# Five-slice feed-forward products: a named place for every weight and split buffer, and a low part ordered behind the first sum

## The chip, the cores and the metric

One Trainium2 chip, one of its cores. The metric is the device time of one execution in microseconds (us). The kernel before takes 1798.35 us, the median of three runs (1797.55 to 1800.99).

## The reference

A decoder block on x (256 tokens, width 2048, float32): a SwiGLU feed-forward of width 5632 added at half weight, a mixer, a second feed-forward, a final norm. The change is about the feed-forwards:

```
def swiglu_ffn(x, w_gate, w_up, w_down):
    return (jax.nn.silu(x @ w_gate) * (x @ w_up)) @ w_down

x = x + 0.5 * swiglu_ffn(rms_norm(x, ffn1_norm), ffn1_w_gate, ffn1_w_up, ffn1_w_down)
z = rms_norm(x, mix_norm) @ w_in            # mixer: two head groups read z
x = x + y @ w_out                           # y: the two normalised groups
x = x + 0.5 * swiglu_ffn(rms_norm(x, ffn2_norm), ffn2_w_gate, ffn2_w_up, ffn2_w_down)
return rms_norm(x, final_norm)
```

## The kernel before

**How a weight is multiplied.** TensorE takes float32 as fp32r, so every weight tile is split in two: `parts_of` (L242) lets ScalarE cast it to fp32r in two pieces (the high part, `hi`), and VectorE subtract (the low part, `lo`). A product of a tile needs two passes with `hi` and one with `lo` for each slice of 128 rows. The weights come from HBM by DMAs issued on SP's queue. All instructions that go through the wrapper of an engine carry line 43 in the profile, so they are told apart by their tiles.

**A product of seven.** `seven` (L454) multiplies a quadrant block of weights w11, w12, w21, w22 (each some slices of 128 rows by 512 columns) with seven products in place of eight, p0 to p6, in the manner of Strassen and Winograd. Beside them stand plain products of further rows, x01, x11, x00, x10, with the weights b2, b3, a2, a3. Sums of weights are formed in place: VectorE adds w12 to w11 (the first sum, L499), then w22 (L524), then w21. GpSimd issues accumulating DMAs, w12 += w22 (L502), in two pieces where there are more than four slices. Only p6 reads that sum. There are four banks of sums, a, c, e, d. The order on TensorE is p0 into a, p4 into c, x01, p5 into a, x11, p6 into a, p2 into c, x00, p3 into a, x10, p1 into d. ScalarE takes snapshots of the banks between products: s1 and u2, u3 of a, and s5 of c, which must be taken before x01 and x11 add into c.

**Stages.** Each feed-forward runs through s = 0 to 4. In stage 0 a gate and an up product run over tall quadrants of four slices (three split pairs). In stages 1 and 2, and again 3 and 4, the quadrants are five slices tall and the plain products three (the "fine" stages, `tall` and `short`, two split pairs). After stages 0, 2 and 4 a down stage uses what was made. So there are 16 five-slice products: in each feed-forward the gate and up products of stages 1 and 2 (a block), a down stage, those of stages 3 and 4 (a second block), and a down stage. The names in the trace are `g`, `u` and `d` with the suffix `_p` for the seven and `_x` for the plain ones.

**Places.** The code asks for buffers from pools of the tile framework. `open_stage` (L184) opens one pool on each side of the on-chip memory; `raw_tile` (L195) takes a weight's place under a tag with two or three buffers ("kept" for w11 and w12, "raw", or "tall" and "short" in the fine stages), and `split_tiles` (L223) takes a pair of hi and lo. Within a tag, the buffer that comes free first is given out; the load into it waits for its last readers. Instructions of an engine are put into an order by the framework's scheduler, except where the kernel asks for program order (`held`, `pinned`).

```
        product_of(0, w11, a, True)
        dve.tensor_tensor(w11, w12, w11, op=ALU.add)
        for h in (slice(0, UK), slice(UK, w12.shape[1])):
            if h.start < h.stop:
                nc.gpsimd.dma_start(w12[:, h, :], w22[:, h, :], accum_op=ALU.add)
        ...
        product_of(4, w11, c, True)
        ...
        s5 = snap(c, "s5")
        ...
        usual(0, b2, 1, (e, 1, True, not two), (c, 0, False, False), first=blk)
```

Of the kernel before, what the change touches and what calls it, by code (L numbers as in the profile page):

```python
# [23 lines left out]
CW = 512  # L24
NC_D = D // CW
UK = 4
NH = 8
# [22 lines left out]
def hybrid_block(ctx: ExitStack, tc: tile.TileContext, a: dict, out: bass.AP):  # L50
    nc = tc.nc
    Engine.pinned = False
    dve, act, pe, sp = (Engine(tc, e) for e in (nc.vector, nc.scalar, nc.tensor, nc.sync))
# [24 lines left out]
    bigs = ctx.enter_context(tc.tile_pool(name="bigs", bufs=10, side="left"))  # L78
# [7 lines left out]
    def f32(ap):  # L86
        return ap.bitcast(F32)
# [82 lines left out]
    def big(name):  # L170

        return bigs.tile([P, UK, 2 * S], F32R, tag="big", name=name)
# [2 lines left out]

    extra = []
    turn_of = {"split": 0}
    stage = {"count": 0}

    def more_from(pool):  # L180
        extra.append(pool)
        turn_of["split"] = 0

    def open_stage(pairs, fine=False):  # L184

        n = stage["count"] = stage["count"] + 1
        for side in ("left", "right"):
            stage[side] = tc.alloc_tile_pool(name=f"stage{n}_{side}", bufs=1, side=side, reuse_waits="tile")
        stage.update(pairs=pairs, fine=fine)

    def close_stage():
        for side in ("left", "right"):
            stage[side].release()

    def raw_tile(name, rows, kept):  # L195
        if kept and extra:
            pool, tag, bufs = (bigs, "big", 10) if extra[0] is bigs else (extra[0], "kept", 2)
        elif kept:
            pool, tag, bufs = stage["right"], "kept", 2
        elif not stage["fine"]:  # L200
            pool, tag, bufs = stage["right"], "raw", 3
        else:
            pool, tag, bufs = stage["right"], "tall" if rows > UK else "short", 2
        return pool.tile([P, rows, CW], F32, tag=tag, name=f"raw_{name}", bufs=bufs)

    def load(src, name, pieces=((0, UK),), loaded=None):
        raw = raw_tile(name, UK, False)
# [6 lines left out]
    def gather(w, cs, runs, name, kept=False):  # L214

        raw = raw_tile(name, sum(n for _, n in runs), kept)
        at = 0
        for k, n in runs:
            sp.dma_start(raw[:, at : at + n, :], w[k * P : (k + n) * P, cs].rearrange("(j p) c -> p j c", p=P))
            at += n  # L220
        return raw

    def split_tiles(name, rows=UK):  # L223
        both = ("hi", "lo")
        if stage["fine"] and rows < UK:
            return [big(f"{part}_{name}")[:, :rows, :] for part in both]
        pool, bufs = stage["left"], stage["pairs"]
        if extra:
            turn_of["split"] += 1
            if turn_of["split"] % 3 == 0:  # L230
                if extra[0] is bigs:
                    return [big(f"{part}_{name}") for part in both]
                pool, bufs = extra[0], 1
        return [pool.tile([P, rows, CW], F32R, tag=part, name=f"{part}_{name}", bufs=bufs) for part in both]

    def low_part(raw, hi, lo):
        dve.tensor_tensor(lo, raw, f32(hi), op=ALU.subtract)

    def blocks(hi, lo):
        return [(hi[:, j, :], lo[:, j, :]) for j in range(hi.shape[1])]  # L240

    def parts_of(raw, name):  # L242
# [211 lines left out]
    def seven(w, rows, cols, sf, xs, name, keep, done, between=None, early=False, own=None, factor=None):  # L454
# [14 lines left out]
        def get(runs, n, kept=False):  # L469
            return gather(w, slice(cols[n], cols[n] + CW), runs, f"{name}_{runs[0][0]}{n}", kept)  # L470
# [16 lines left out]
        def usual(i, raw, n, *targets, first=None):  # L487

            blk = first or parts_of(raw, f"{name}_x{i}{n}")
            if own:  # L490
                last = i == len(xs) - 1
                targets = [(apart[t, n], t, i == 0, last) for t in range(NT)]
            multiply([(ps, xs[i][1](t), b, z) for ps, t, b, z in targets], blk, True)
            if own and last:
                for t in range(NT):
                    own(t, n, apart[t, n])

        product_of(0, w11, a, True)
        dve.tensor_tensor(w11, w12, w11, op=ALU.add)  # L499
        for h in (slice(0, UK), slice(UK, w12.shape[1])):  # L500
            if h.start < h.stop:
                nc.gpsimd.dma_start(w12[:, h, :], w22[:, h, :], accum_op=ALU.add)  # L502
# [3 lines left out]
        blk = None  # L506
        if early:
            between("second product")
            hi, lo = split_tiles(f"{name}_x01")
# [4 lines left out]
            blk = blocks(hi, lo)  # L514
# [13 lines left out]
        blk = blk2 = None  # L528
        if early:
            blk = parts_of(b3, f"{name}_x11")  # L530
# [29 lines left out]
        done(0, 0, d, [s1])  # L560

    def ffn(tag, norm, after, opening=False):
        with tc.tile_pool(name=f"ffn{tag}", bufs=1, side="left") as fp:
            wg, wu, wd = (a[f"ffn{tag}_w_{s}"][0] for s in ("gate", "up", "down"))

            def keep(name, dt=F32):
                return fp.tile([P, CW], dt, tag="keep", name=name, bufs=11)

            def spare_tile(name, dt=F32):
                return stage["right"].tile([P, CW], dt, tag="spare", name=name, bufs=2)  # L570

            open_stage(3)

            hidden = {}
            turned = {}
# [98 lines left out]
            left = []  # L674
# [265 lines left out]
            for s in range(5):  # L940
                cs = (CW + 2 * s * CW, 2 * CW + 2 * s * CW)
# [54 lines left out]
                if s == 0:  # L996
                    fifth()
                else:
                    if s % 2 == 0:
                        close_stage()  # L1000
                        open_stage(3)
                if s % 2 == 0:
                    down(s == 4)
            close_stage()
# [45 lines left out]

    acc = const.tile([P, 2, S], F32, name="acc")
    yT, yv = [], []
    open_stage(2)
    with tc.tile_pool(name="mixer", bufs=1, side="left") as mp, tc.tile_pool(name="mixw", bufs=2, side="left") as mw:
        wgate = {}

        def gate_weights(key, src):
            raw = stage["right"].tile([P, NH, P], F32, tag="raw", name=f"rawgate_{key}", bufs=3)
# [9 lines left out]
        zx, gv, hs, vs, ds, ts, cc, ys, yh, xcs = ({} for _ in range(10))  # L1068

        def tmp(tag, name, w=S, dt=F32, bufs=2):  # L1070
            return mw.tile([P, w], dt, tag=tag, name=f"{tag}_{name}", bufs=bufs)

        def halves(ps, name):

# [151 lines left out]
        def sc_c(between):  # L1226
# [35 lines left out]
                    turn(1)  # L1262

            c0 = 3 * (D // 2)
            more_from(bigs)
# [33 lines left out]
        behind = None  # L1299
        for i, (use, part, half) in enumerate(order):  # L1300
            ps = columns(w_in, part * (D // 2) + half * CW, nm.xT, f"in_{part}_{half}", behind)
            behind = None
            if i == 0:
# [5 lines left out]
                behind = sc_c(lambda: use(ps, half))  # L1309
# [28 lines left out]
        n2.later(0)  # L1338


    with tc.tile_pool(name="outs", bufs=1, side="left") as op:
        more_from(op)

        def snapshot(name):
            return op.tile([P, CW], F32, tag="snap", name=name, bufs=4)

        so = {}
        pair = [big(f"ys_{i}") for i in range(2)]
# [40 lines left out]
        extra.clear()  # L1389
    close_stage()  # L1390


    fss = const.tile([P, NT, NC_D], F32, name="fss")
# [96 lines left out]
```

## Time and profile before

| | |
|---|---|
| time, median of 3 | 1798.35 us |
| the profiled execution | 1795.43 us |
| its span | 1793.7 us |
| mean granted clock of TensorE | 0.988 |
| TensorE busy | 1734.6 us, 97% |
| VectorE busy | 1500.4 us, 84% |
| ScalarE busy | 1088.8 us, 61% |
| bytes moved by DMA | 376.81 MB, 210 GB/s |

A row of a timeline gives the start, the duration (of several instructions in a row, "x4", from the first start to the last end), the engine, the line, the operation, the tile written and the tiles read, the shape, and in brackets the idle time of the engine before it with what ended it. A row of the waits gives the total, the number and the longest. A row of the stretches gives the busy time of each engine in a stretch of the span, TensorE's granted clock, the DMA engines' share and GB/s. Matmuls are pipelined: a group's time runs past the start of the next one, so the pitch is read from start to start.

### The profile page before, as it was taken

What the parts mean: (1) busy time and instruction counts of PE and PEld (TensorE: products, weight loads), DVE (VectorE), ACT (ScalarE), POOL (GpSimd) and SP (SyncE); (2) the same over time, 40 slices, a digit from 0 to 9 for tenths busy, and PEclk for the clock granted to TensorE, in tenths of its full rate; (3) what the DMA queues carried; (4) which work ended last, traced back from release to release, by engine and by line L of the source; (5) the groups of instructions that cost most, each with busy time, mean ns of one, the idle gap of its engine ahead of it and who ended that gap; (6) DMA issues with size and microseconds to landing.
All of it is one profiled execution on the core that took longest, in us unless ns stands there. A gap on an engine that the chain in (4) does not pass through costs nothing.

```text
span 1793.7 us, 20426 instructions
## 1 busy us (share of the span) xinstructions
PE 1734.6 (97%) x7937; PEld 1428.7 (80%) x7937; DVE 1500.4 (84%) x1226; ACT 1088.8 (61%) x1408; POOL 47.7 (3%) x78
## 2 busy tenths in 40 slices
PE   9999799999999999999999989999899999999998
PEld 8888688788788788888888868887678788787776
DVE  7988689889589888787997878897889885998896
ACT  7665366556465656667866656654566563656564
POOL 0100000000000000000000000000000000000000
PEclk9999899999999999999999999999999999999999
DMA  8774586656677665565556555673877576877483
GB/s 305 244 241 150 179 279 200 217 202 202 221 226 228 205 223 176 211 189 191 184 189 223 179 187 186 217 252 127 273 236 220 154 236 211 268 222 235 125 274 118
DMA packets 181586, 376.81 MB, mean 210 GB/s; under 512 B 7412, under 2 KB 10352, under 8 KB 177776
## 3 DMA queue, kind: packets, MB, share of 16 engines
q1 hardware_dynamic: 174656, 340.81, 54.5%
q0 software_dynamic: 6656, 33.63, 10.0%
q8 instruction: 62, 1.02, 0.2%
q10 hardware_dynamic: 176, 1.06, 0.1%
q14 instruction: 36, 0.29, 0.0%
HBM read 339.82 MB, written 2.10 MB: 191 GB/s over the span
## 4 chain that ended last, share of the span: by engine, by line
PE 89%; DVE 4%; DMA 3%; ACT 2%; issue 1%; SPq 0%; DVEq 0%; POOL 0%; ACTq 0%; POOLq 0%
PE ps_d L43 11%; PE ps_in L43 10%; PE ps_u_a L43 9%; PE ps_g_a L43 9%; PE ps_u_c L43 6%; PE ps_g_c L43 6%; PE ps_d_a L43 5%; PE ps_u_d L43 4%; PE ps_d_c L43 3%; PE ps_g_d L43 3%; PE ps_g L43 3%; PE ps_u_e L43 2%; PE ps_o L43 2%; PE ps_d_d L43 2%; PE ps_u L43 2%; PE ps_g_e L43 2%
## 5 line engine op out<-in xcount | busy, mean ns | idle before, releaser
L43 ACT CAST hi_g_p<-raw_g 128x1024 fp32r<-128x1024 f32 (+2 forms) x139 | 164.2, 1228 | 120.1 <-DVE raw_g L43 35.9
L43 DVE TENSOR_TENSOR lo_u_p<-raw_u,hi_u_p 128x2560 fp32r<-128x2560 f32 (+1 forms) x70 | 189.0, 2713 | 50.6 <-ACT hi_u_p L43 50.6
L43 DVE TENSOR_TENSOR lo_g_p<-raw_g,hi_g_p 128x2560 fp32r<-128x2560 f32 (+1 forms) x70 | 189.4, 2714 | 46.2 <-ACT hi_g_p L43 46.1
L43 ACT CAST hi_u_p<-raw_u 128x1024 fp32r<-128x1024 f32 (+1 forms) x140 | 163.7, 1216 | 52.4 <-DVE raw_u L43 37.2
L43 PE MATMUL ps_d<-hi_d,h 128*128 128x512 f32 x696 | 166.4, 390 | 0.0
L43 PEld LDWEIGHTS ps_d<-hi_d,h 128*128 128x128 f32 x696 | 129.8, 188 | 26.8
L43 PE MATMUL ps_in<-xT_nm,hi_in 128*128 128x512 f32 x512 | 122.6, 391 | 1.6 <-ACT hi_in L43 1.6
L43 ACT CAST hi_d<-raw_d 128x1024 fp32r<-128x1024 f32 x88 | 87.8, 1050 | 44.8 <-DMA raw_d<-in_ffn_w_down_dram 14.0
L43 DVE TENSOR_TENSOR lo_d<-raw_d,hi_d 128x2048 fp32r<-128x2048 f32 x44 | 100.3, 2288 | 16.3 <-ACT hi_d L43 15.4
L43 PEld LDWEIGHTS ps_in<-xT_nm,hi_in 128*128 128x128 f32 x512 | 94.0, 188 | 20.8 <-ACT hi_in L43 2.1
L43 ACT CAST hi_d_p<-raw_d 128x1024 fp32r<-128x1024 f32 x84 | 84.2, 1046 | 41.5 <-DVE raw_d L43 34.8
L43 DVE TENSOR_TENSOR lo_d_p<-raw_d,hi_d_p 128x2048 fp32r<-128x2048 f32 x42 | 95.3, 2287 | 13.6 <-ACT hi_d_p L43 13.5
L43 DVE TENSOR_TENSOR lo_in<-raw_in,hi_in 128x2048 fp32r<-128x2048 f32 x32 | 73.2, 2286 | 20.6 <-ACT hi_in L43 20.2
L43 PE MATMUL ps_d<-lo_d,h 128*128 128x512 f32 x348 | 86.8, 391 | 0.3
L43 DVE TENSOR_TENSOR raw_u<-raw_u,raw_u 128x2560 f32<-128x2560 f32 (+1 forms) x30 | 81.4, 2713 | 1.0 <-DMA raw_u<-in_ffn_w_up_dram 0.7
L43 DVE TENSOR_TENSOR raw_g<-raw_g,raw_g 128x2560 f32<-128x2560 f32 (+1 forms) x30 | 81.4, 2714 | 0.7 <-DMA raw_g<-in_ffn_w_gate_dram 0.2
L43 ACT CAST hi_u_x<-raw_u 128x1024 fp32r<-128x1024 f32 x80 | 67.3, 873 | 23.1 <-DMA raw_u<-in_ffn_w_up_dram 19.3
L43 ACT CAST hi_in<-raw_in 128x1024 fp32r<-128x1024 f32 x64 | 64.0, 1046 | 26.2 <-PE ps_in L43 17.0
L43 DVE TENSOR_TENSOR lo_g_x<-raw_g,hi_g_x 128x1536 fp32r<-128x1536 f32 (+1 forms) x40 | 74.3, 1857 | 3.7 <-ACT hi_g_x L43 3.7
L43 PEld LDWEIGHTS ps_d<-lo_d,h 128*128 128x128 f32 x348 | 65.0, 188 | 15.4 <-DVE lo_d L43 2.0
L43 DVE TENSOR_TENSOR lo_u_x<-raw_u,hi_u_x 128x1536 fp32r<-128x1536 f32 (+1 forms) x40 | 74.2, 1856 | 0.0
L43 ACT CAST hi_g_x<-raw_g 128x512 fp32r<-128x512 f32 (+2 forms) x79 | 66.6, 888 | 5.8 <-PE ps_g_c L43 2.3
(491 smaller groups left out, 3812.5 us busy)
## 6 DMA issues: line engine op xcount, KB each, us to landing
raw_d<-in_ffn_w_down_dram SPq DMA_DIRECT2D x88, 1024.0 KB, 5.2
raw_u<-in_ffn_w_up_dram SPq DMA_DIRECT2D x55, 1024.0 KB, 5.3
raw_g<-in_ffn_w_gate_dram SPq DMA_DIRECT2D x54, 1024.0 KB, 6.6
raw_in<-in_w_in_dram SPq DMA_DIRECT2D x32, 1024.0 KB, 5.0
raw_g<-in_ffn_w_gate_dram SPq DMA_DIRECT2D x32, 768.0 KB, 8.6
raw_u<-in_ffn_w_up_dram SPq DMA_DIRECT2D x32, 768.0 KB, 6.4
raw_g<-raw_g POOLq DMA_DIRECT2D x10, 1024.0 KB, 7.7
raw_u<-raw_u POOLq DMA_DIRECT2D x10, 1024.0 KB, 7.0
```

What stands on the lines that cost most here:

```text
L43: ins = getattr(self.engine, name)(*args, **kwargs)
```

## The change

Three things. The pools become many pools of one place each, listed in `layouts`, and each tile of a fine stage names its place: w11 kept0, w12 kept1, b2 and a2 short0, b3 and a3 short1, w22 tall1, w21 tall2. In the other stages the raw places and everywhere the split pairs are handed out in rotation, the least recent first (`least_recent`), with a list of pairs set by hand for one part of the down stage (`plan`). In the fine stages the low part of b2 (x01) gets a dependence without a semaphore on the first sum, so that it is issued behind it on VectorE (`issue_behind`). The mixer's temporary buffers are divided among three pools, the feed-forwards', mixer's and out stage's pools are opened with `reuse_waits="tile"`, the out stage opens a layout of its own, and it has ten places for snapshots in place of four. What is computed stays the same.

```diff
+    layouts = {
+        "three": (["pair0", "pair1", "pair2"], ["raw2", "raw1", "raw0", "kept", "spare"]),
+        "two": (["pair0", "pair1"], ["raw2", "raw1", "raw0"]),
+        "fine": (["pair0", "pair1"], ["short1", "tall1", "short0", "kept1", "kept0", "tall2"]),
+    }
+
+    def open_stage(layout, raws=None):
+
+        n = len(opened) + 1
+        left, right = layouts[layout]
+        for side, names in (("left", left), ("right", right)):
+            for name in names:
+                pools[name] = pool_of(f"{name}_{n}", side, 2 if name in ("kept", "spare") else 1)
+        if raws:
+            recent["raw"] = deque(raws)
+        recent["pair"] = deque([i for i in recent["pair"] if i < len(left)] + [i for i in range(len(left)) if i not in recent["pair"]])
+        opened.append(layout)
...
+    def least_recent(kind):
+        i = plan.popleft() if kind == "pair" and plan else recent[kind][0]
+        recent[kind].remove(i)
+        recent[kind].append(i)
+        return f"{kind}{i}"
+
+    def raw_tile(name, rows, role=None):
+        if role in ("kept0", "kept1") and not fine():
+            if extra:
+                return bigs.tile([P, rows, CW], F32, tag="big", name=f"raw_{name}")
+            return pools["kept"].tile([P, rows, CW], F32, tag="kept", name=f"raw_{name}", bufs=2)
+        where = role if fine() else least_recent("raw")
+        return pools[where].tile([P, rows, CW], F32, tag="raw", name=f"raw_{name}")
...
     def split_tiles(name, rows=UK):
         both = ("hi", "lo")
-        if stage["fine"] and rows < UK:
+        turn_of["split"] += 1
+        if fine() and rows < UK or extra and turn_of["split"] % 3 == 0:
             return [big(f"{part}_{name}")[:, :rows, :] for part in both]
...
+        pool = pools[least_recent("pair")]
+        return [pool.tile([P, rows, CW], F32R, tag=part, name=f"{part}_{name}") for part in both]
...
+    def issue_behind(ins, first):
+
+        why = mybir.DependencyInfo(mybir.DependencyClass.NoSync, mybir.DependencyReason.DATA)
+        tc.add_manual_dep(ins.ins, first.ins.name, why, reason="behind")
...
-        low_part(raw, hi, lo)
+        ins = low_part(raw, hi, lo)
+        if first is not None:
+            issue_behind(ins, first)
         return blocks(hi, lo)
...
-        w11, w12 = get(r0, 0, True), get(r0, 1, True)
-        b2, w22 = get(xs[0][0], 1), get(r1, 1)
-        b3 = get(xs[1][0], 1) if two else None
-        a2, w21 = get(xs[0][0], 0), get(r1, 0)
-        a3 = get(xs[1][0], 0) if two else None
+        w11, w12 = get(r0, 0, "kept0"), get(r0, 1, "kept1")
+        b2, w22 = get(xs[0][0], 1, "short0"), get(r1, 1, "tall1")
+        b3 = get(xs[1][0], 1, "short1") if two else None
+        a2, w21 = get(xs[0][0], 0, "short0"), get(r1, 0, "tall2")
+        a3 = get(xs[1][0], 0, "short1") if two else None
...
         product_of(0, w11, a, True)
-        dve.tensor_tensor(w11, w12, w11, op=ALU.add)
+        first_sum = dve.tensor_tensor(w11, w12, w11, op=ALU.add)
...
-        usual(0, b2, 1, (e, 1, True, not two), (c, 0, False, False), first=blk)
+        usual(0, b2, 1, (e, 1, True, not two), (c, 0, False, False), first=blk, after=first_sum if fine() else None)
...
                 for c in (0, 3):
+                    if c == 3:
+                        others = [i for i in recent["pair"] if i != 2]
+                        plan.extend(others + others[: len(us) - 3] + [2])
...
                 if s % 2 == 1:
                     close_stage()
-                    open_stage(2, True)
+                    open_stage("fine")
+                    recent["pair"] = deque(range(2))
...
-                        open_stage(3)
+                        open_stage("three", (1, 0, 2))
+                        recent["pair"] = deque(range(3))
...
+        mixa = mixer.enter_context(tc.tile_pool(name="mixa", bufs=2, side="left", reuse_waits="tile"))
+        open_stage("two")
+        mixer.callback(close_stage)
+        mixb = mixer.enter_context(tc.tile_pool(name="mixb", bufs=2, side="left", reuse_waits="tile"))
+        mixc = mixer.enter_context(tc.tile_pool(name="mixc", bufs=2, side="left", reuse_waits="tile"))
...
-    with tc.tile_pool(name="outs", bufs=1, side="left") as op:
-        more_from(op)
+    with tc.tile_pool(name="outs", bufs=1, side="left", reuse_waits="tile") as op:
+        open_stage("three")
 
         def snapshot(name):
-            return op.tile([P, CW], F32, tag="snap", name=name, bufs=4)
+            return op.tile([P, CW], F32, tag="snap", name=name, bufs=10)
```

More of the change, by code (lines that the diff above doesn't have):

```diff
@@ L195, in raw_tile @@
[L195 to L204, printed above, removed]
+    pools = {}
@@ new lines, in hybrid_block, with pool_of @@
+    recent = {"raw": deque(range(3)), "pair": deque(range(3))}
+    plan = deque()
+    opened = []
+    def pool_of(name, side, bufs=1):
+        return tc.alloc_tile_pool(name=name, bufs=bufs, side=side, reuse_waits="tile")
+    layouts = {
[3 more added lines that the diff above has]
+    }
@@ new lines, in close_stage, with fine @@
+    def close_stage():
+        left, right = layouts[opened[-1]]
+        for names in (left, right):
+            for name in reversed(names):
+                pools.pop(name).release()
+    def fine():
+        return opened[-1] == "fine"
+    def least_recent(kind):
[10 more added lines that the diff above has]
+        return pools[where].tile([P, rows, CW], F32, tag="raw", name=f"raw_{name}")
@@ L212, in load, with gather @@
         return raw
-    def gather(w, cs, runs, name, kept=False):
-        raw = raw_tile(name, sum(n for _, n in runs), kept)
+    def gather(w, cs, runs, name, role):
+        raw = raw_tile(name, sum(n for _, n in runs), role)
         at = 0
@@ L224, in split_tiles, with parts_of @@
         both = ("hi", "lo")
-        if stage["fine"] and rows < UK:
+        turn_of["split"] += 1
+        if fine() and rows < UK or extra and turn_of["split"] % 3 == 0:
             return [big(f"{part}_{name}")[:, :rows, :] for part in both]
[L227 to L234, printed above, removed]
+        pool = pools[least_recent("pair")]
+        return [pool.tile([P, rows, CW], F32R, tag=part, name=f"{part}_{name}") for part in both]
     def low_part(raw, hi, lo):
-        dve.tensor_tensor(lo, raw, f32(hi), op=ALU.subtract)
+        return dve.tensor_tensor(lo, raw, f32(hi), op=ALU.subtract)
+    def issue_behind(ins, first):
+        why = mybir.DependencyInfo(mybir.DependencyClass.NoSync, mybir.DependencyReason.DATA)
+        tc.add_manual_dep(ins.ins, first.ins.name, why, reason="behind")
     def blocks(hi, lo):
         return [(hi[:, j, :], lo[:, j, :]) for j in range(hi.shape[1])]
-    def parts_of(raw, name):
+    def parts_of(raw, name, first=None):
         rows = raw.shape[1]
@@ L485, in product_of, with usual @@
             multiply([(ps, sf[i], begin, end)], blk or parts_of(raw, f"{name}_p{i}"), True)
-        def usual(i, raw, n, *targets, first=None):
-            blk = first or parts_of(raw, f"{name}_x{i}{n}")
+        def usual(i, raw, n, *targets, first=None, after=None):
+            blk = first or parts_of(raw, f"{name}_x{i}{n}", after)
             if own:
@@ L1052, in hybrid_block @@
     yT, yv = [], []
-    open_stage(2)
-    with tc.tile_pool(name="mixer", bufs=1, side="left") as mp, tc.tile_pool(name="mixw", bufs=2, side="left") as mw:
+    with ExitStack() as mixer:
+        mixa = mixer.enter_context(tc.tile_pool(name="mixa", bufs=2, side="left", reuse_waits="tile"))
[3 more added lines that the diff above has]
+        mixc = mixer.enter_context(tc.tile_pool(name="mixc", bufs=2, side="left", reuse_waits="tile"))
+        home = {tag: mixa for tag in ("v", "d", "T", "xs", "ysq")}
+        home.update({tag: mixc for tag in ("half", "y", "g2")})
         wgate = {}
         def gate_weights(key, src):
-            raw = stage["right"].tile([P, NH, P], F32, tag="raw", name=f"rawgate_{key}", bufs=3)
+            raw = pools[least_recent("raw")].tile([P, NH, P], F32, tag="raw", name=f"rawgate_{key}")
             nc.sync.dma_start(raw, src.rearrange("h i j -> i h j"))
```

31 lines of the change are left out of this document (10 added, 21 removed).

## The prediction

> **What bounds the kernel now.** I read the engines' busy shares first, then the waits of TensorE, then the stretches of the span by stage, and last the order in time of one product.
>
> ```profile
> PE 1734.6 (97%) x7937; PEld 1428.7 (80%) x7937; DVE 1500.4 (84%) x1226; ACT 1088.8 (61%) x1408; POOL 47.7 (3%) x78
> PE ps_g_c L43 <- ACT hi_g_p L43: 13.6, 5, 3.3
> PE ps_u_c L43 <- ACT hi_u_p L43: 9.6, 5, 2.3
> PE ps_g L43 <- ACT hi_g L43: 7.6, 2, 7.0
> ```
>
> The first line is the page's part 1, the others TensorE's waits (total, times, longest us). TensorE is the bound; all that another order can win is its idle 3% and its slow restarts. The waits lie where the change works: the starts of the five-slice stages (the g sums, FFN2's first `ps_g`) and the first up product of two stages (the u sums). By stage:
>
> ```profile
> core 0: us, PE busy (x) PEld busy (x) DVE busy (x) ACT busy (x) POOL busy (x), PEclk, DMA share, GB/s
> 200.50:384.80 184.30, 171.72 (x735) 138.66 (x734) 155.60 (x86) 108.21 (x122) 7.00 (x8) 0.96 0.72 228
> 471.00:647.80 176.80, 169.30 (x734) 136.50 (x733) 155.39 (x85) 108.12 (x122) 7.03 (x8) 0.98 0.70 215
> 1255.30:1436.80 181.50, 170.27 (x734) 136.08 (x734) 155.38 (x85) 108.69 (x122) 7.03 (x8) 0.98 0.71 223
> 1522.50:1697.40 174.90, 167.48 (x733) 135.24 (x732) 155.34 (x85) 106.61 (x121) 7.03 (x8) 0.99 0.70 216
> ```
>
> These are the four five-slice blocks: each two gate and two up products, 16 in all, 717.5 us together. VectorE has some 155 of 175 to 184 us of work in each, so it can wait little before TensorE waits for it. One product in its steady state, ScalarE, VectorE, GpSimd and the landing of the accumulating DMAs:
>
> ```profile
> 519.90 1.05 ACT L43 CAST hi_u_p<-raw_u 128x1024 fp32r<-128x1024 f32 x1 [3.05 <-DVE raw_u L43]
> 521.39 1.46 ACT L43 CAST hi_u_p<-raw_u 128x1536 fp32r<-128x1536 f32 x1
> 527.23 0.60 ACT L43 ACTIVATE s_u<-ps_u_c 128x512 f32<-128x512 f32 x1 [3.88 <-PE ps_u_c L43]
> 528.66 4.75 ACT L43 CAST hi_u_p<-raw_u 128x1024 fp32r<-128x1024 f32 x4 [0.83 <-DVE raw_u L43]
> 516.98 2.82 DVE L43 TENSOR_TENSOR raw_u<-raw_u,raw_u 128x2560 f32<-128x2560 f32 x1
> 531.11 5.56 DVE L43 TENSOR_TENSOR lo_u_p<-raw_u,hi_u_p 128x2560 fp32r<-128x2560 f32 x2 [2.55 <-ACT hi_u_p L43]
> 520.47 1.76 POOL L502 DMA_DIRECT2D raw_u<-raw_u  x2 [40.57 <-DVE s_g L43]
> 561.81 1.75 POOL L502 DMA_DIRECT2D raw_g<-raw_g  x2 [39.58 <-DVE raw_g L43]
> ...
> raw_u<-raw_u POOLq DMA_DIRECT2D x1, 1024.0 KB, 7.7
> raw_u<-raw_u POOLq DMA_DIRECT2D x1, 256.0 KB, 9.6
> ```
>
> Call the end of the first sum T0, here 516.98 + 2.82 = 519.8. GpSimd issues the accumulation of w22 into w12 at T0+0.67; it has landed, both pieces, at T0+10.3. Only p6 reads it. ScalarE takes the snapshot s5 at T0+7.4 and casts p5 and then p6 from T0+8.9 without a gap, so the accumulation is hidden here. The period is 561.81 - 520.47 = 41.3 us.
>
> **The change part by part.** *1. The order inside a five-slice product.* The built order of the changed program, the same in all 16 sevens, against before (an up product):
>
> ```
> ACT before  ... s1, s5, hi.p5, hi.p6, hi.x00, hi.p2, u2 ...
> ACT after   ... s1, hi.p4, hi.x11, hi.p6, s5, hi.p5, hi.x00, hi.p2, u2 ...
> DVE before  lo.p0, lo.x01, first sum, lo.x11, lo.p4, second sum, lo.p5, lo.p6 ...
> DVE after   lo.p0, first sum, lo.x01, lo.p4, lo.x11, second sum, lo.p6, lo.p5 ...
> ```
>
> The first sum goes ahead of `lo.x01`, which is what `issue_behind` says. But p6's cast now stands ahead of s5 and of p5's casts on ScalarE, which runs in order, and it needs the accumulation. Queued behind it are s5, p5, x00 and p2; TensorE needs s5 before x01 may add into bank c, and its order there (x01 into c, x11, p5, p6) has not moved. So s5 is due at 0.67 + 9.6 + 1.46 + 0.60 = T0+12.3 instead of T0+7.4. TensorE has at T0 about 2.8 us of p0 left, then p4 and x01 into e, and stands at T0+8.3: a stall of about 4 us in each product.
>
> The price is the period of the loop that this closes. TensorE's own price:
>
> ```profile
> 383.65 1.30 PE L43 MATMUL ps_u_d<-lo_u_p,x 128*128 128x512 f32 x5
> 384.78 3.58 PE L43 MATMUL ps_d<-hi_d,h 128*128 128x512 f32 x15
> 546.73 2.82 DVE L43 TENSOR_TENSOR lo_u_p<-raw_u,hi_u_p 128x2560 fp32r<-128x2560 f32 x1
> 549.47 1.75 DVE L43 TENSOR_TENSOR lo_u_x<-raw_u,hi_u_x 128x1536 fp32r<-128x1536 f32 x1
> 549.62 5.28 SPq L43 DMA_DIRECT2D raw_g<-in_ffn_w_gate_dram  x5
> raw_u<-in_ffn_w_up_dram SPq DMA_DIRECT2D x55, 1024.0 KB, 5.3
> ```
>
> 5 matmuls take 1.13 us, 0.227 each (15 to a p, 18 to an x: 7 and 4 of them are 40.1 us). A 128x2560 pass of VectorE takes 2.74 from start to start. From T0: s5 at 12.3; 36 matmuls (x01 into c, x11, p5) 8.2; p2's casts, which need p5's pair and stand ahead of u2 on ScalarE, and u2, 2.4 + 0.6; p6 3.4; p3, which needs p6's pair, cast 2.4, low part 2.8; the next w11, cast and split 7.8 + 2.7 + 2.7 (next point). Sum 45.4. With the landings of the four products of a block (below), 45.2.
>
> *2. A fixed place for each weight.* Before, w11 of the next product took the place that came free first, w12's, and w12 took w11's, where it is needed only by the first sum. Now w11 has a place of its own, kept0, and its load waits for `lo.p3` of the product before. From the end of `lo.p3` (549.5; the load is issued at 549.62): load 5.3, casts 2.5, low part 2.7, sum 2.7: T0 can be no earlier than 13.2 after. Before it was 11.6 (the issue at 561.81 less 0.67, less 549.5). Behind this load on SP's queue stand w21, a2 and a3 of the same product, needed much later. Alone this costs up to 1.5 us of lead, all of it in the loop above; the loads that no longer wait for each other are no gain where T0 waits for the latest.
>
> *3. The starts of the stages.* Pools with several places each made the first weights of a five-slice stage wait for the stage before:
>
> ```profile
> 198.78 1.98 PE L43 MATMUL ps_d<-lo_d,h 128*128 128x512 f32 x8
> 207.10 4.64 PE L43 MATMUL ps_g_a<-hi_g_p,x 128*128 128x512 f32 x10 [6.34 <-ACT hi_g_p L43]
> 200.79 2.33 SPq L43 DMA_DIRECT2D raw_g<-in_ffn_w_gate_dram  x4
> 200.79 0.69 DVE L43 SCALAR_TENSOR_TENSOR xres<-ps_d,xres 128x512 f32<-128x512 f32 x1 [0.21 <-PE ps_d L43]
> 215.58 1.74 POOL L502 DMA_DIRECT2D raw_g<-raw_g  x2 [66.00 <-ACT hi_g_x L43]
> 257.44 1.75 POOL L502 DMA_DIRECT2D raw_u<-raw_u  x2 [40.12 <-DVE s_g L43]
> ```
>
> The load stood until the last matmul of the down stage; in the new order it waits for an earlier low part. What is then late is the first sum, which stays behind the two updates of `xres`: 0.7 + 2.8, T0 about 4.0 after the last matmul (in the first block before: 214.9 - 200.8 = 14.1). Add 0.8 for a block's first period, which runs on weights that are still arriving: in the first block it was 257.44 - 215.58 = 41.9, against 41.3 above. A block then takes 4.0 + 0.8 + 4 x 45.2 = 185.6; four take 742.4: **+24.9** against 717.5. The gains at the stages' starts and of the first sum in the up products are inside this figure.
>
> *4. Restarts.* After a stall TensorE runs slowly:
>
> ```profile
> 344.41 1.21 PE L43 MATMUL ps_u_c<-hi_u_p,xs 128*128 128x512 f32 x4 [2.29 <-ACT hi_u_p L43]
> 345.46 1.08 PE L43 MATMUL ps_u_e<-hi_u_x,x 128*128 128x512 f32 x3
> 479.25 2.07 PE L43 MATMUL ps_g_c<-hi_g_p,xs 128*128 128x512 f32 x4 [3.08 <-ACT hi_g_p L43]
> 481.13 1.47 PE L43 MATMUL ps_g_e<-hi_g_x,x 128*128 128x512 f32 x3
> 479.00:483.00 4.00, 3.75 (x10) 2.98 (x11) 3.44 (x2) 3.04 (x4) 0.90 (x1) 0.57 1.02 197
> ```
>
> Undisturbed, 5 show 1.30 (at 383.65), so 4 would show 1.07 and 3 some 0.85. After 2.29 us idle the two rows lose 0.14 + 0.23 = 0.4, after 3.08 they lose 1.0 + 0.6 = 1.6, and the granted clock of that stretch is 0.57. Ends for a new stall: 0 and 1.6; I take 0.8, since some stalls will be shorter than 4 us: 16 x 0.8 = **+12.8**.
>
> *5. Outside the blocks.* The weights of FFN2's first product and of the mixer's first are cast ahead of the norm's tail and the squares in the new order:
>
> ```profile
> 1059.64 4.67 PE L43 MATMUL ps_g<-hi_g,xT_n 128*128 128x512 f32 x13 [6.97 <-ACT hi_g L43]
> 737.97 3.92 PE L43 MATMUL ps_in<-xT_nm,hi_in 128*128 128x512 f32 x16 [1.63 <-ACT hi_in L43]
> ```
>
> I take off 1.6 for the mixer and 7.5 for FFN2's start (6.97 idle, and 13 matmuls in 4.67 where 13 x 0.227 is 3.0; the norm's tail stays), and put 1.0 on for the down products of two stages, where p6 moves ahead too: **-8.1**. Bounds: 0 (another input is as late as the weights) and the whole of the rows, -10.3. The ten snapshot places and the split mixer pools cost nothing: the out stage and the mixer show TensorE busy throughout; without that cover a snapshot is 0.6.
>
> Sum: 24.9 + 12.8 - 8.1 = +29.6 on the profiled execution's 1795.4 (its span is 1793.7): 1825.0. That execution lies 2.9 below the median 1798.35, so **1828**.
>
> **The rivals.** *Every restart at half speed.* If all 16 stalls exceed 3 us, each costs the 1.6 of 479.25, 12.8 more: 1841. For it: the stall worked out is 4. Against: early landings make it shorter. [...]
>
> *The accumulation lands early, not slower.* Place: the cast of p6. Landings by product:
>
> ```profile
> raw_u<-raw_u POOLq DMA_DIRECT2D x1, 256.0 KB, 7.8
> ...
> raw_u<-raw_u POOLq DMA_DIRECT2D x1, 256.0 KB, 10.5
> ```
>
> 7.8 is the second up product of a block, where no load ran beside it; 10.5 the first up of the first block. At 7.8 everywhere the period is 45.4 - 1.8 = 43.6, the stall 2.3, the restart near 0: blocks 4 x 179.2 = 716.8, and -8.1 elsewhere: 1786.6, with the offset 1789.5. It decides when the second piece lands by about 8 us everywhere; against it, the loads of a2, w21 and a3 still run at that time. At 10.5 everywhere the period is 46.3 and the time 1846.
>
> *The loop has slack.* If next product's loads and pairs come free sooner than I have them, the stall alone counts: 40.1 + 4.4 = 44.5 and no restart: 4 x 182.8 = 731.2, +13.7 - 8.1, with the offset 1804.
>
> *It does what it says.* If p6's cast ahead of s5 costs nothing, every block is 4.8 + 4 x 41.3 = 170, -37.5 - 8.1: 1753. For that the accumulation would have to land at T0+6; no row comes near.
>
> **How the numbers follow.** Forecast 0.45; half-speed restarts or late landings 0.22; early landing 0.15; slack 0.13; as intended 0.05. About 0.2% (3.6 us) is what a measurement of this kernel can tell from no change. Faster is early landing and as intended, 0.20; same is half of the slack case, 0.07; slower the rest, 0.73. The range runs from just below the early landing, 1786, to the late one, 1846; the likeliest case's own, with restarts from 0 to 1.6 each, is 1815 to 1841.
>
> **What would show it.** In the profile after: TensorE waits of 3 to 4.5 us for ScalarE's s_g and s_u ahead of `ps_g_c` and `ps_u_c`, 16 of them; ScalarE idle ahead of a 128x1536 cast of `hi_p`, released by a DMA of raw into itself; GpSimd's accumulations 44 to 47 us apart within a block; granted clock below 0.9 in slices of the blocks. The waits of 6.3 at 207 and 7.0 at 1059 gone. It is wrong if the accumulations are 42 us apart, if s5 is ahead of its bank's need, or if the lost time stands in the mixer or the down stages.

## The result, and the profile after

The changed kernel takes 1859.25 us (median of 4 runs, 1855.91 to 1865.93) against 1797.95 us: 1.0346 times the kernel before, 95% interval 1.0312 to 1.038. It was forecast slower, at 1828 with a range up to 1846; it is slower by twice as much as forecast. The profiled execution has a span of 1856.8 us, 63.1 more than before.

From the page of the changed kernel, part 1, and then its waits of TensorE (total, times, longest us):

```profile
PE 1755.4 (95%) x7937; PEld 1450.4 (78%) x7937; DVE 1502.2 (81%) x1226; ACT 1095.8 (59%) x1408; POOL 45.7 (2%) x78
PE ps_u_c L43 <- ACT s_u L43: 34.8, 8, 4.5
PE ps_g_c L43 <- ACT s_g L43: 32.2, 8, 6.0
PE ps_g_c L43 <- ACT hi_g_p L43: 11.1, 8, 2.6
PE ps_u_c L43 <- ACT hi_u_p L43: 10.5, 5, 2.7
```

The 16 waits for the snapshots s_g and s_u are there, one in each five-slice product, 67.0 us together, 4.2 each (about 4 was worked out). Below them stand 13 waits for casts, 21.6 us. Eight of them, about 2.6 us each, are for p4, which follows the first sum: in the first gate and the first up product of each block. The rest are short. TensorE's busy time has grown by 20.8 us with the same 7937 matmuls, at a lower granted clock (0.972 on average, 0.988 before): slow restarts. The old waits of 6.3 us at the first stage's start and 7.0 us at the second feed-forward's are gone.

The four blocks in the stretches of the changed kernel (columns as before):

```profile
202.10:397.80 195.70, 175.16 (x734) 141.69 (x734) 156.07 (x87) 107.64 (x120) 6.99 (x8) 0.94 0.67 203
483.60:681.80 198.20, 174.55 (x734) 141.47 (x733) 156.65 (x87) 108.73 (x120) 7.03 (x8) 0.94 0.66 200
1280.10:1476.80 196.70, 174.84 (x734) 141.30 (x733) 155.93 (x87) 109.14 (x122) 7.03 (x8) 0.94 0.67 202
1562.30:1760.30 198.00, 175.19 (x733) 141.53 (x732) 155.75 (x87) 107.34 (x119) 7.02 (x8) 0.94 0.66 201
```

They take 788.6 us against 717.5: 71.1 more. The rest of the span is 1068.2 against 1076.2: 8.0 less. So all of the loss lies in the blocks (the five-slice stages between two down stages), and the granted clock there has fallen from 0.96 to 0.99 down to 0.94.

One product in the second block of the changed kernel, timelines of GpSimd, VectorE, ScalarE and TensorE:

```profile
535.06 2.82 DVE L43 TENSOR_TENSOR raw_u<-raw_u,raw_u 128x2560 f32<-128x2560 f32 x1
538.46 1.76 POOL L525 DMA_DIRECT2D raw_u<-raw_u  x2 [47.30 <-ACT hi_u_x L43]
546.37 1.05 ACT L43 CAST hi_u_p<-raw_u 128x1024 fp32r<-128x1024 f32 x1 [5.47 <-DMA raw_u<-raw_u]
548.95 1.47 ACT L43 CAST hi_u_p<-raw_u 128x1536 fp32r<-128x1536 f32 x1 [1.53 <-DMA raw_u<-raw_u]
550.32 0.59 ACT L43 ACTIVATE s_u<-ps_u_c 128x512 f32<-128x512 f32 x1
550.97 2.92 PE L43 MATMUL ps_u_c<-hi_u_x,x 128*128 128x512 f32 x6 [4.44 <-ACT s_u L43]
569.57 2.82 DVE L43 TENSOR_TENSOR lo_u_p<-raw_u,hi_u_p 128x2560 fp32r<-128x2560 f32 x1
577.74 2.43 ACT L43 CAST hi_g_p<-raw_g 128x1024 fp32r<-128x1024 f32 x2 [6.34 <-DMA raw_g<-in_ffn_w_gate_dram]
580.98 0.69 DVE L43 TENSOR_TENSOR z<-ps_u_a,z 128x512 f32<-128x512 f32 x1 [3.45 <-PE ps_u_a L43]
581.58 2.82 DVE L43 TENSOR_TENSOR lo_g_p<-raw_g,hi_g_p 128x2560 fp32r<-128x2560 f32 x1
584.32 1.28 DVE L43 TENSOR_TENSOR h<-ph,h 128x512 fp32r<-128x512 f32 x2
585.51 2.82 DVE L43 TENSOR_TENSOR raw_g<-raw_g,raw_g 128x2560 f32<-128x2560 f32 x1
588.92 1.75 POOL L525 DMA_DIRECT2D raw_g<-raw_g  x2 [48.70 <-DVE s_u L43]
635.23 1.75 POOL L525 DMA_DIRECT2D raw_u<-raw_u  x2 [44.55 <-DVE s_g L43]
```

Two things are to be read here. First, ScalarE idles twice ahead of p6's casts, released by the accumulating DMA, and only then takes the snapshot s5: it ends at 550.91, 13.0 after the first sum ended (537.88), and TensorE has waited 4.44 us for it. Second, the low part of p3 (569.57) ends at 572.39; then the next w11 loads into the same place, is cast (577.74), and has its low part (581.58) and the next first sum (585.51, ends at 588.33). That is 15.9 us, with a z and two h of the product before in VectorE's queue between; over the 12 periods inside the blocks it is 14.7 on average (13.6 to 16.0). The periods are 588.92 - 538.46 = 50.5 and 46.3 us.

### The profile page after: what moved, and what is told of

It is laid out like the page before. It is cut to its first block, busy times and chain, and to the rows that moved or that the text cites. A ratio compares the mean times of both kernels' runs of the same rounds, so it can differ in the third digit from the quotient of the medians.

```text
span 1856.8 us, 20381 instructions
## 1 busy us (share of the span) xinstructions
PE 1755.4 (95%) x7937; PEld 1450.4 (78%) x7937; DVE 1502.2 (81%) x1226; ACT 1095.8 (59%) x1408; POOL 45.7 (2%) x78
## 5 line engine op out<-in xcount | busy, mean ns | idle before, releaser
L43 DVE TENSOR_TENSOR lo_u_p<-raw_u,hi_u_p 128x2560 fp32r<-128x2560 f32 (+1 forms) x70 | 189.8, 2716 | 85.0 <-ACT hi_u_p L43 80.5
L43 ACT CAST hi_g_p<-raw_g 128x1024 fp32r<-128x1024 f32 (+2 forms) x139 | 164.8, 1226 | 136.3 <-DMA raw_g<-raw_g 47.6
L43 ACT CAST hi_d<-raw_d 128x1024 fp32r<-128x1024 f32 x88 | 87.0, 1046 | 70.0 <-DMA raw_d<-in_ffn_w_down_dram 33.8
L43 PE MATMUL ps_u_c<-hi_u_x,x 128*128 128x512 f32 x128 | 43.5, 489 | 34.8 <-ACT s_u L43 34.8
```

What stands on the lines that cost most here:

```text
L43: ins = getattr(self.engine, name)(*args, **kwargs)
```

## The experiments

The expectations name two theories first: P, that p6's cast ahead of s5 is the cost, as the prediction had it; W, that the fixed place of w11 sets the period. Each ratio is to the kernel before, with its 95% interval.

**Each part undone by itself.** The first run orders p6 behind s5 and p5 in the changed kernel; `split_of` and `snapped` hold the casts and the snapshots.

```diff
...
         def product_of(i, raw, ps, begin=False, end=True, blk=None):
-            multiply([(ps, sf[i], begin, end)], blk or parts_of(raw, f"{name}_p{i}"), True)
+            blk = blk or parts_of(raw, f"{name}_p{i}")
+            if i == 6 and fine():
+                five, six = (split_of[f"{name}_p{k}"] for k in (5, 6))
+                for cast in six[:2]:
+                    for first in (snapped["s5"], five[0], five[1]):
+                        issue_behind(cast, first)
+                issue_behind(six[2], five[2])
+            multiply([(ps, sf[i], begin, end)], blk, True)
```

> The changed kernel, with the casts of p6 ordered behind s5 and behind p5's casts on ScalarE, and p6's low part behind p5's on VectorE, in the 16 five-slice products. Theory P (the cast of p6 ahead of s5 is the cost): the 16 waits for s_g and s_u and their restarts (about 4.2 and 1.4 us each) go, the periods fall from 46 to 51 us to about 42, and the time to 1755 to 1780, below the kernel before. Rival W (the fixed place of w11 and its late load set the period): the waits for s_g and s_u go, others take their place, and the time stays above 1820.

Measured: 1845.25 us, 1.0268 (1.0244 to 1.0291). Theory P falls as the whole cause: only 14 us come back. Its waits of TensorE:

```profile
PE ps_g_c L43 <- ACT hi_g_p L43: 22.2, 8, 3.0
PE ps_u_c L43 <- ACT hi_u_p L43: 20.6, 10, 2.6
PE ps_u_a L43 <- ACT hi_u_p L43: 12.1, 6, 3.4
PE ps_u_a L43 <- DVE lo_u_p L43: 10.1, 9, 1.3
```

The 4.2 us waits for the snapshots are gone (the few for s_u that are left are 0.7 at most, as before). In their place TensorE waits for p4, which follows the first sum, and for p0 and p5. With p6 out of the way the first sum is still late.

The second run lets w11 and w12 change places from product to product, so that w11 loads into the place that p6 has left:

```diff
-        w11, w12 = get(r0, 0, "kept0"), get(r0, 1, "kept1")
+        turn_of["kept"] = 1 - turn_of.get("kept", 1)
+        one = turn_of["kept"]
+        w11, w12 = get(r0, 0, f"kept{one}"), get(r0, 1, f"kept{1 - one}")
```

> The changed kernel, with w11 and w12 taking kept0 and kept1 in turn from product to product, so that the next w11 loads into the place that the low part of p6 frees. Theory P: little, 1845 to 1860, since s5 still waits for the accumulation. Rival W: the load of w11 is no longer late, the periods fall to 42 to 44 us and the time to 1790 to 1820.

Measured: 1819.66 us, 1.0123 (1.0097 to 1.0148). 40 us come back, at the edge of what W expected, though all 16 waits for the snapshots remain (52.8 us together in its trace).

The third run takes the dependence alone into the kernel before; the fourth takes it out of the changed one (`after=None` in the call of `usual` for x01).

> The kernel before, with the low part of x01 issued behind the first sum in the five-slice products, and nothing else of the change. Theory P (the order of p6 comes from the places, not from this): the four stalls of 2.3 us with their restarts at the first up product of stages 2 and 4 go, 4 x 3 to 4 us: about 1783 to 1788. Rival: it is this dependence that costs, 1815 or more.

Measured: 1801.58 us, 1.0022 (1.0009 to 1.0034): no gain, if anything a small loss. The expected gain was there and was given back: the stalls of 2.3 us in the up products of stages 2 and 4 are gone, but in the up products of stages 1 and 3 TensorE now waits 2.4 to 3.3 us for p5. ScalarE and TensorE in one of these:

```profile
533.74 1.04 ACT L43 CAST hi_u_x<-raw_u 128x1024 fp32r<-128x1024 f32 x1 [4.32 <-DMA raw_u<-in_ffn_w_up_dram]
534.69 4.74 ACT L43 CAST hi_u_p<-raw_u 128x1024 fp32r<-128x1024 f32 x4
535.78 1.20 PE L43 MATMUL ps_u_a<-hi_u_p,xs 128*128 128x512 f32 x4 [2.40 <-ACT hi_u_p L43]
```

The second sum ends at 531.72, 10.3 us after the first (8.8 before), since x01's and x11's low parts now stand between them on VectorE. And the built order puts x00's cast, which waits for its load, ahead of p5's on ScalarE, so that p5 starts only at 534.69.

> The changed kernel without the dependence of x01's low part on the first sum. Theory P: p6's cast still stands ahead of s5, so 1850 to 1870. Rival (this dependence costs): 1800 to 1830.

Measured: 1854.63 us, 1.0317 (1.0296 to 1.0338). Taking the dependence out brings 5 of the 61 us back, so it isn't what made the change slow.

**Both parts undone together.** After these runs the theory was L: two loops stand beside each other, each long enough by itself, so that cutting one shows the other.

> The changed kernel with both edits of the earlier runs: p6's casts behind s5 and p5, and w11 and w12 in kept0 and kept1 in turn. Theory L (two loops of about 46 us stand beside each other: the late s5, and the load of w11 behind the low part of p3; each alone keeps the period up): with both cut the period is 41.5 to 43 us and the time 1765 to 1785. Rival A (the two add up): 1859 - 14 - 40 = 1805 or more.

Measured: 1785.83 us, 0.9936 (0.9919 to 0.9954). 73 us come back, more than 14 + 40. This speaks for L and against rival A, just past the end of the window given.

The next run gets at p6 in another way. It takes the two split pairs of the five-slice stages from one pool of two, first free first, in place of the rotation; in its built order s5 and p5 stand ahead of p6 with no dependence asked for.

```diff
-        "fine": (["pair0", "pair1"], ["short1", "tall1", "short0", "kept1", "kept0", "tall2"]),
+        "fine": (["pair0"], ["short1", "tall1", "short0", "kept1", "kept0", "tall2"]),
...
     def split_tiles(name, rows=UK):
...
+        if fine():
+            return [pools["pair0"].tile([P, rows, CW], F32R, tag=part, name=f"{part}_{name}", bufs=2) for part in both]
         pool = pools[least_recent("pair")]
```

> The changed kernel with the two split pairs of the five-slice stages taken from one pool of two, the first that is free, as before, in place of a fixed rotation; w11 stays in kept0. In its built order s5 and p5 stand ahead of p6 again. Theory L: only one loop is cut, periods of 46 to 50 us, 1830 to 1850, with waits for hi_g_p and hi_u_p in place of those for s_g and s_u. Rival A: about 1845; a time under 1815 would say that the rotation of the pairs was the cause by itself.

Measured: 1853.41 us, 1.0315 (1.0296 to 1.0333), 3 us over the window of L. As in the first run, p6 is out of the way (the waits for s_u that are left are 0.7 at most), and the time hardly falls. So the rotation of the pairs is where p6's early cast came from, and it isn't the cause by itself.

> The changed kernel with the pairs from one pool of two and w11, w12 in turn: the two parts of the change undone that theory L names, all else of it kept. Theory L: 1765 to 1785, faster than the kernel before by the starts of the stages and of the second feed-forward. Rival A: 1800 or more.

Measured: 1800.57 us, 1.0015 (1.0006 to 1.0024): 59 us come back where 6 + 40 would be the sum, but the window of L is missed by 16, and the time lies where rival A had it (1800 or more). Both loops are cut here as in the run at 1785.83, so the difference between the two must come from the other things that the pool of pairs changes; the table below shows where it stands. The next run asks for the dependence's part.

> As the run before, without the dependence of x01's low part on the first sum. That dependence alone, in the kernel before, moved the stall of the first up products from p4 to p5. Theory L: within 8 us of the run before. If the dependence is worth what its four stalls showed, 10 to 14 us slower than it.

Measured: 1781.46 us, 0.9916 (0.9897 to 0.9934). The dependence in all 16 products costs 19 us here, outside both guesses, against 5 in the changed kernel and 4 in the kernel before. L would say that an order off the loop that sets the period hardly counts; that fits the changed kernel, but in the kernel before neither loop stands and the cost is as small, so this comparison doesn't decide.

**The disputed cost by itself.** One line in the kernel before gives w11 and w12 a place each in the five-slice stages (the two tiles are asked for with `kept` 1 and 2):

```diff
-            pool, tag, bufs = stage["right"], "kept", 2
+            pool, tag, bufs = stage["right"], f"kept{kept}" if stage["fine"] else "kept", 1 if stage["fine"] else 2
```

> The kernel before with one part of the change alone: in the five-slice stages w11 always takes one place and w12 another, in place of the first that is free. Theory L (the load of w11 behind the low part of p3 is a loop of its own, of 46 to 50 us): 16 periods longer by 4 to 6 us, 1850 to 1880 less what the slack at the stages' starts takes: 1840 to 1870. The price of the prediction (up to 1.5 us of lead in each product): 1798 to 1822.

Measured: 1834.54 us, 1.0209 (1.0192 to 1.0226), 37 us more than before by this alone, with p6 in its old order. The prediction's price allowed 1822 at most; L's 1840 was a little high. Timelines of GpSimd, VectorE, SP's queue, ScalarE and TensorE of this run:

```profile
527.93 2.82 DVE L43 TENSOR_TENSOR raw_u<-raw_u,raw_u 128x2560 f32<-128x2560 f32 x1
531.34 1.76 POOL L502 DMA_DIRECT2D raw_u<-raw_u  x2 [43.47 <-DVE raw_u L43]
558.16 2.82 DVE L43 TENSOR_TENSOR lo_u_p<-raw_u,hi_u_p 128x2560 fp32r<-128x2560 f32 x1
561.04 5.29 SPq L43 DMA_DIRECT2D raw_g<-in_ffn_w_gate_dram  x5
566.39 1.05 ACT L43 CAST hi_g_p<-raw_g 128x1024 fp32r<-128x1024 f32 x1 [7.74 <-DMA raw_g<-in_ffn_w_gate_dram]
566.64 0.69 DVE L43 TENSOR_TENSOR z<-ps_u_a,z 128x512 f32<-128x512 f32 x1 [1.25 <-PE ps_u_a L43]
567.76 1.07 ACT L43 CAST h<-ph 128x512 fp32r<-128x512 f32 x2 [0.32 <-PE ph L43]
568.38 1.29 DVE L43 TENSOR_TENSOR h<-ph,h 128x512 fp32r<-128x512 f32 x2 [1.05 <-ACT h L43]
568.72 1.49 ACT L43 CAST hi_g_p<-raw_g 128x1536 fp32r<-128x1536 f32 x1
570.25 2.83 DVE L43 TENSOR_TENSOR lo_g_p<-raw_g,hi_g_p 128x2560 fp32r<-128x2560 f32 x1 [0.58 <-ACT hi_g_p L43]
572.99 0.68 DVE L43 TENSOR_TENSOR s_u<-ps_u_d,s_u 128x512 f32<-128x512 f32 x1
573.59 2.82 DVE L43 TENSOR_TENSOR raw_g<-raw_g,raw_g 128x2560 f32<-128x2560 f32 x1
577.00 1.75 POOL L502 DMA_DIRECT2D raw_g<-raw_g  x2 [43.89 <-DVE raw_g L43]
577.59 2.08 PE L43 MATMUL ps_g_c<-hi_g_p,xs 128*128 128x512 f32 x4 [2.59 <-ACT hi_g_p L43]
```

Here is the loop by itself. From one first sum, which ends at 530.75, to the end of p3's low part, 560.98, are 30.2 us, about what it was before (519.8 to 549.5). The load of the next w11 is issued 0.06 later. The load, the two casts with one of h between them on ScalarE, the low part, s_u and the sum end at 576.4: 15.4 more. The period is 45.7 and TensorE waits 2.59 us for p4. Over the 12 periods inside the blocks, the first stretch averages 31.0 us before and 31.2 here, the second 12.2 before and 14.8 here: the whole growth stands between p3's low part and the next first sum.

**A version that beats both.** The stalls that the dependence cures are in the first gate and the last up product of each block. The next three runs ask for it only there, in four or eight products (the first two with the pool of pairs and w11, w12 in turn, as above): `after=first_sum` where the product is an up of stage 2 or 4, and in the last two also a gate of stage 1 or 3.

> As the run with the pairs from one pool, w11 and w12 in turn and no dependence, with the dependence put back in the first-up products of stages 2 and 4 alone, the four with the stall of 2.3 us at p4. If a stall cut there stays cut: 4 x 2.5 us faster, about 1771. If it moves on to p5 as it did in the kernel before: 1779 to 1784.

Measured: 1775.40 us, 0.9877 (0.9862 to 0.9892): 6 us faster than without, between the two guesses. TensorE's waits for p4 in the up products fell from 9.3 to 0.8 us.

> As the run before this, with the dependence also in the first gate product of each block, where the first sum stands behind the low part of x01 and TensorE waits 4 us for p4. If both kinds of stall stay cut: 1760 to 1768. If p5 is late in its place: 1770 to 1785.

Measured: 1784.74 us, 0.9928 (0.9913 to 0.9943): a loss of 9 us against the run before, in the upper window.

> The changed kernel with p6's casts behind s5 and p5, w11 and w12 in turn, and the dependence in the same eight products only. With theory L and the stalls of the other eight (p5 late by 1.5 to 2.2 us with the dependence) gone: 1762 to 1775. Rival: the dependence cost nothing there, 1784 to 1788 as with it in all 16.

Measured: 1767.48 us, 0.9833 (0.9818 to 0.9847), the fastest. It keeps the named places, the early starts of the stages and the rotation of the pairs; p6 is ordered behind s5 and p5, w11 and w12 change places, and the dependence is asked for in eight products. From its page and its GpSimd timeline:

```profile
PE 1723.5 (98%) x7937; PEld 1421.7 (81%) x7937; DVE 1499.5 (85%) x1226; ACT 1093.2 (62%) x1408; POOL 45.8 (3%) x78
...
464.98 1.77 POOL L538 DMA_DIRECT2D raw_g<-raw_g  x2 [71.19 <-ACT s_g L43]
510.26 1.76 POOL L538 DMA_DIRECT2D raw_u<-raw_u  x2 [43.51 <-ACT s_u L43]
551.20 1.75 POOL L538 DMA_DIRECT2D raw_g<-raw_g  x2 [39.18 <-DVE raw_g L43]
593.50 1.75 POOL L538 DMA_DIRECT2D raw_u<-raw_u  x2 [40.55 <-DVE s_g L43]
```

The periods of this block are 45.3, 40.9 and 42.3 us, where 40.1 is TensorE's own work. All 12 average 43.0, as good as the 43.2 of the kernel before. So the 30 us that this version gains are hardly in the period.

**Where the time of each run stands.** Each block is split in three: the start, from the end of the down stage's last matmul to the end of the first sum in the block's first product; the three periods from there to the first sums of the next products; and the last product, from the end of its first sum to the next down stage's first matmul. The columns are sums over the four blocks (4 starts, 12 periods, 4 last products), then the rest of the span and the span, in us; rows may be 0.1 off by rounding:

| | starts | periods | last products | rest | span |
|---|---|---|---|---|---|
| before | 34.4 | 518.7 | 163.7 | 1076.9 | 1793.7 |
| changed | 16.2 | 581.9 | 189.8 | 1068.9 | 1856.8 |
| p6 behind | 15.3 | 593.3 | 166.3 | 1067.1 | 1842.0 |
| w11, w12 in turn | 15.8 | 543.7 | 189.6 | 1071.3 | 1820.4 |
| both | 17.0 | 535.3 | 164.7 | 1067.0 | 1784.0 |
| w11 fixed in before | 35.3 | 551.4 | 165.6 | 1078.1 | 1830.5 |
| pool of pairs, w11, w12 in turn | 28.0 | 533.4 | 163.1 | 1072.3 | 1796.8 |
| the same, no dependence | 35.4 | 510.1 | 160.8 | 1071.5 | 1777.8 |
| the same, in four | 35.6 | 503.0 | 163.0 | 1072.8 | 1774.5 |
| the same, in eight | 27.7 | 519.1 | 163.1 | 1073.5 | 1783.3 |
| the fastest | 15.5 | 516.0 | 164.8 | 1067.5 | 1763.8 |

The cost of p6's order shows openly only in the last products, behind which no w11 of a five-slice product loads: 26 us more in the changed kernel, and gone with p6 behind. In the periods, ordering p6 alone brings nothing (593.3 against 581.9). The fixed w11 stands in the periods alone: 33 us more where it is put into the kernel before.

Of the fastest version's 30 us, 19 are in the starts, which the changed kernel has too, 9 outside the blocks and 3 in the periods. The pool of pairs with w11 and w12 in turn (1800.57) loses 11 us in the starts and 5 outside the blocks against the run with both parts undone by the other edit (1785.83); its periods are as short. That is where it missed L's window. The dependence in eight products in place of 16 gains 16 us with the pool of pairs (1800.57 to 1784.74) and 18 with the rotation (1785.83 to 1767.48). With the pool of pairs the step from four to eight gains 8 us in the starts and loses 16 in the periods; why the periods grow was not followed up.

## Why the prediction was wrong

**The order of p6 (step 1): mechanism right.** s5 came 12.7 to 13.8 us after the first sum, 13.0 on average, where 12.3 was worked out, and the 16 waits average 4.2 us where about 4 was said. The difference is the second piece of the accumulation, which is issued after the first: in the product above p6's second cast, released by it, starts 11.1 us after the first sum, where 10.3 was taken for both pieces. But p6's order doesn't carry the time by itself: undone alone it gives 6 to 14 us, and 34 once w11 and w12 change places (1819.66 to 1785.83).

**The fixed place of w11 (step 2): the step that failed.** It was written off as "up to 1.5 us of lead, all of it in the loop above". It is a loop of its own, and undone alone it gives 40 us. Put alone into the kernel before, it costs 37 us, 2.7 in each of the 12 periods. Part of this could be read on the page of before: 29.7 us from a first sum to the end of p3's low part, with nothing stalled, plus the 13.2 of the chain, is 42.9, already 1.6 over the period of 41.3. The difference had been booked as lead, and lead that has to be paid in every product is period. (41.3 is the period of that one product; the 12 of the kernel before run from 41.4 to 46.4 and average 43.2. Against that average, 31.0 + 13.2 is 1.0 over.)

The other part is the size of the chain. 13.2 counts only w11's own load, casts, low part and sum; measured from the end of p3's low part it averages 14.7 in the changed kernel and 14.8 in the run with the fixed place alone, since work of the product before stands in between: z and two h on VectorE in the product of the changed kernel above, a cast of h on ScalarE and s_u on VectorE in the other.

**The loop and its sum.** The 12 periods inside the blocks run from 46.3 to 51.0 us and average 48.5, where 45.2 + 0.8 for a restart was forecast, with 0.8 more for the first of each block: 27 of the 33 us by which the blocks (742.4 + 12.8 = 755.2 forecast, 788.6 measured) came out longer. The last products, 47.5 us from the first sum to the block's end where 46.0 was forecast, are 6 more. Cut at the end of p3's low part, the 12 periods are 33.8 + 14.7 us, where the sum had 32.1 + 0.8 and 13.2. So in each period the forecast's chain behind the fixed place is 1.5 us short, 18 us in the 12, and its way from the first sum to p3, with the restart, 0.9. Chaining the two loops into one, and giving it one price, also left out that the first sum can be late by itself: of TensorE's waits for p4, the four at the starts of the blocks, 10.2, fit the forecast, and the four in the first up products, 10.4, were in no term.

**The starts of the stages (step 3): right.** The first sums end 3.8 to 4.7 us after the down stages; 4.0 was said. Two readings beside it were off and cost little: in the first block before, the first sum ended at 214.14, 0.8 earlier than was taken from the issue at 215.58, and 41.9 against 41.3 is 0.6, not the 0.8 that was added.

**Restarts (step 4): mis-sized.** 0.8 each was taken between 0 and 1.6. Counted as the time beyond 0.227 us for each matmul until the pace is back, the 16 waits for snapshots lost 0.1 to 3.0 us, 1.9 on average and 30 in all, where 12.8 was forecast. The first of the two stretches below is behind the wait that ends at 550.97 in the changed kernel; 15 matmuls, 3.4 us at 0.227 each, took 5.99 at a granted clock of 0.56 (the 16th of the count starts where the stretch ends).

```profile
550.97:556.96 5.99, 5.99 (x16) 4.69 (x17) 5.99 (x3) 3.81 (x4) 0.00 (x0) 0.56 0.42 125
346.40:349.40 3.00, 3.00 (x9) 2.33 (x8) 2.97 (x2) 0.00 (x0) 0.00 (x0) 0.51 1.09 218
```

The second, in the kernel before, shows where the low price came from: after the stall of 2.29 us that ends at 344.41 the prediction looked at two rows, up to 346.4, and read a loss of 0.4. The slow stretch came behind them, at a granted clock of 0.51, and the whole loss is 1.8. So the rival with the slow restarts was nearer; its 1841 still lacks step 2. A restart lies on the way from the first sum to p3, so these 17 us are in part the 0.9 of the paragraph above and can't be added to it.

**Outside the blocks (step 5): right.** -8.1 forecast, -8.0 measured.

Of the rivals, early landing failed on its own condition: the second piece landed 10.7 to 11.8 us after the first sum, not about 8. The change doing what it says failed on the 16 waits, and slack on the second loop, which had none. All three also took that loop to be short.

## What to carry to other kernels

Where a buffer gets a fixed address, follow the loop that this closes: from the buffer's last reader through the load to the next use, and on to that last reader again, with all that stands in the engines' queues on the way. Each such loop is compared with the period by itself, since the longest sets the time; cutting one of two loops of like length can show little (14 of 73 us here), and the worth of each part is read only with the other cut. A dependence or an address that changes nothing of the work still changes the order that a scheduler builds: read the built order of every engine for what now stands ahead of what.

## What the runs showed of the hardware

In these traces the length of a short stall alone didn't set the price of the restart. Two of TensorE's stalls of like length in the changed kernel, and then the granted clock (the column after GpSimd's) in the stretches behind them:

```profile
489.72 1.21 PE L43 MATMUL ps_g_c<-hi_g_p,xs 128*128 128x512 f32 x4 [2.56 <-ACT hi_g_p L43]
539.06 3.68 PE L43 MATMUL ps_u_c<-hi_u_p,xs 128*128 128x512 f32 x8 [2.60 <-ACT hi_u_p L43]
...
489.60:493.60 4.00, 3.88 (x17) 3.19 (x18) 3.03 (x2) 1.97 (x3) 1.56 (x2) 1.00 0.71 135
539.00:543.00 4.00, 3.94 (x10) 3.14 (x11) 3.13 (x2) 1.90 (x3) 1.22 (x2) 0.57 0.84 164
```

After 2.56 us the clock stayed at 1.00; after 2.60 it was 0.57, and eight matmuls took 3.68 us where 8 x 0.227 is 1.8. In the traces of before, of the changed kernel, of its first two edits, of the fixed w11 and of the fastest version, counted as above, the stalls of 1.0 to 1.8 us lost 0.6 at most. Of the 49 between 1.8 and 2.75 us, 17 lost 0.4 at most and 32 lost 1.5 to 2.3. All 47 longer ones lost 1.4 to 3.3. What makes the difference between two stalls of one length, no trace here shows.
